# Four staging places in turn: where the block chunks of a down projection keep their output rows

## The chip, the cores and the metric

The kernel runs on one core of one Trainium2 chip. The metric is the time of one execution in microseconds (us) on the device. TensorE multiplies, VectorE (DVE in the profile) and ScalarE (ACT) do the work between the products, GpSimd (POOL) issues the transfers that accumulate, SyncE (SP) the plain ones.

## The reference, cut to what matters

One decoder layer runs on 576 tokens (512 of a prompt, 64 of a sample group): a combined Mamba2 and mLSTM mixer, a cross-attention over 256 memory rows, and a SwiGLU network. All is float32. The change touches only the last product of the last part:

```python
u = _rms(x) * g_pre_ffn
f = (jax.nn.silu(u @ w_gate) * (u @ w_up)) @ w_down      # 1024 -> 2816 -> 1024
x = x + _rms(f) * g_post_ffn
```

## The kernel before, in words

Activations lie with features on the 128 partitions and tokens along the free axis. Every float32 product is made of three: each operand is split into a high part, a cast to the fp32r type, and a low part, what the cast left over; a product is high times high, high times low and low times high (lines 1860 to 1862 for the down projection). So each weight tile and each operand needs a cast on ACT (line 192) and a difference on DVE (line 193).

The hidden width is 22 tiles of 128. The gated rows are made in pairs of tiles (`Pair`, called by the number of the pair's first tile: 4, 6, 8, ... 20). A pair multiplies 2x2 blocks with seven products instead of eight, the two 288-token halves `E[0]` and `E[1]` being one of the two block axes. The gate values of one pair are four blocks of 128x288 in the tile `gt`, which has room for two pairs: `gates(j)` returns half `j // 2 % 2` of it. When a pair is done, `place` forms differences of its four blocks (line 1611) and splits them into the operand tile `hop`.

The down projection runs in four pieces over the hidden axis. The middle two are the block chunks, `down_blocks(1)` behind pair 8 and `down_blocks(2)` behind pair 14. Each takes three operand tiles and gives all eight output rows of 128 features, as four blocks of two rows: `Down(c, n_)` for `n_` 0 to 3 is called block 0 to block 3 here. A block

- loads its weights into a `raw` and a `rawx` buffer (line 1821, on SP; two buffers of each, which `Pair` uses too, at lines 1651 and 1655),
- forms sums and differences of them (lines 1837 and 1611) and splits the results into `whi`/`wlo`, `wacc` and `u3h`/`u3l`,
- runs seven products of nine matmuls each, products 0 to 6, in up to three PSUM banks,
- moves intermediate banks out with `keep` (ACT, line 1865) into the small tiles `cc` and `ct`, and adds them to a later bank with `plus` (DVE, line 1868), whose result goes into the block's *staging rows* `s.st`: three of the four results of a block come by `plus`, the fourth is a copy on ACT (line 1907),
- adds the two staging rows to the sum in device memory, `f2_d`, with two accumulating transfers (`store`, line 1914, on POOL).

Block n's products 5 and 6 (`late`) come in the program after block n+1's products 0 and 1 (`early`). `Pair` objects are prepared in the same way around it, so the work of the first gated pair behind a chunk (pair 10 behind chunk 1, pair 16 behind chunk 2) is mixed into its last blocks.

Blocks 0 and 2 stage in two buffers of the tag "ssq" (tile `fst`), blocks 1 and 3 in one half of `gt`: that of the last pair ahead of the chunk, `gates(6 * c + 2)`, pair 8 for chunk 1 and pair 14 for chunk 2. A staging place that is used again waits until the transfers out of it have landed.

The order of the instructions in this part of the program is set by the tile scheduler from its own estimate of times, engine by engine; on the chip every engine then takes its instructions strictly in that order. Transfers issued from one engine start in that engine's order as well. One more user of the tag "ssq" follows: the tile `ssqf` for the last piece, whose padding POOL clears (line 1023) and which takes over the buffer of whichever block used the tag last.

The names in the profile: `ps_dn` is a PSUM bank of the down projection, `ps_g` and `ps_u` are those of a gated pair, `f_d` is `f2_d`.

Of the kernel before, what the change touches and what calls it, by code (L numbers as in the profile page):

```python
# [116 lines left out]
def build(nc, tc, ctx, I, O):  # L117
# [187 lines left out]
    for k in range(KT):  # L305
        if k % 2 == 0:
            c = slice(128 * k, 128 * k + 256)
# [1328 lines left out]
    def gates(j):  # L1636

        return [[gt[:, 4 * (j // 2 % 2) + 2 * a + i, :] for i in range(2)] for a in range(2)]
# [6 lines left out]
    class Pair:  # L1645

        def __init__(s, j, up, dst):
            s.j, s.up, s.dst, s.first = j, up, dst, not up and j in (10, 16)
            s.src = I["wup" if up else "wgate"]
            s.r1 = wp.tile([P, 1024], F32, name="raw", tag="raw", bufs=2)  # L1650
            S.dma_start(s.r1, s.src[j])
# [162 lines left out]
    class Down:  # L1814

        def __init__(s, c, n_):
            s.c, s.j = c, 2 * n_
            s.r1 = wp.tile([P, 1024], F32, name="raw", tag="raw", bufs=2)[:, :768]
            s.r2 = fp.tile([P, 1024], F32, name="rawx", tag="rawx", bufs=2)[:, :768]
            for a, r in enumerate((s.r1, s.r2)):  # L1820
                S.dma_start(r, I["wdown"][s.j + a, :, 768 * c - 256:768 * c + 512])
            if n_ % 2:
                g4 = gates(6 * c + 2)
                s.st = [[g4[a][i] for i in range(2)] for a in range(2)]
                s.rows = [gt[:, 4 * ((3 * c + 1) % 2) + 2 * a:4 * ((3 * c + 1) % 2) + 2 * a + 2, :].rearrange("p i t -> p (i t)") for a in range(2)]
            else:
                s.rows = [ph.tile([P, 640], F32, name="fst", tag="ssq", bufs=2)[:, :T] for _ in range(2)]
                s.st = [[r[:, c_] for c_ in E] for r in s.rows]
# [144 lines left out]
    with tc.manual_schedule(engines={TE.engine, A.engine, V.engine, G.engine, S.engine}):  # L1973
# [5 lines left out]
        gt = fp.tile([P, 8, 288], F32, name="gt")  # L1979
# [263 lines left out]
```

## Time and profile before

| | us |
|---|---|
| Median of 3 runs | 1169.33 (1166.7 to 1169.33) |
| The profiled execution | 1174.03 |
| its span, first to last instruction | 1172.2 |
| TensorE busy in the span | 1118.5 (95%), 8355 matmuls |
| DVE, ACT, POOL busy | 756.5 (65%), 619.8 (53%), 232.8 (20%) |
| Mean granted TensorE clock | 0.978 of full speed |

By stage, in us from the start of the span:

| stretch | what runs | TensorE busy | granted clock |
|---|---|---|---|
| 0 to 865 | everything up to pair 8 | 849.09 of 865 | 0.99 |
| 865 to 945 | chunk 1, start of pair 10 | 65.78 of 80 | 0.88 |
| 945 to 995 | pairs 10 to 14 | 50.00 of 50 | 0.99 |
| 995 to 1085 | chunk 2, pairs 16 and 18 | 72.69 of 90 | 0.89 |
| 1085 to 1172.2 | pair 20, last piece, output | 80.93 of 87.2 | 0.99 |

The busy time of TensorE is that of matmuls whose ends are modelled, so a full stretch is one without gaps, not one at peak. In the table the gaps stand in two places, the two block chunks. The third part of a timeline row in brackets is the idle time of the engine just before the instruction and what ended it.

### The profile page before, as it was taken

The numbers are of one execution on the slowest core, as the hardware profiler recorded it, in microseconds if no ns is written. First come the engines' busy times: TensorE is split into PE (matmuls) and PEld (weight loads), VectorE is DVE, ScalarE is ACT, GpSimd is POOL, SyncE is SP. The second block draws the span as 40 slices with busy tenths as digits, with TensorE's granted clock in tenths as the row PEclk, the third lists the DMA queues.
The fourth block names the chain that finished last, engine by engine and source line by source line (L and its number), as shares of the span: only waits on it lengthen the run. The fifth ranks groups of instructions, "written<-read, shape, count | busy, mean of one in ns | idle before, by whom it ended". The sixth has DMA issues, their size and how long they took to land.

```text
span 1172.2 us, 21300 instructions
## 1 busy us (share of the span) xinstructions
PE 1118.5 (95%) x8355; PEld 1062.3 (91%) x8355; DVE 756.5 (65%) x1503; ACT 619.8 (53%) x1148; POOL 232.8 (20%) x319
## 2 busy tenths in 40 slices
PE   9999999999999999999999999999998899778997
PEld 8999898898998999899888899999987899778997
DVE  6897773567766865677544556665583578554655
ACT  6877432445643656555444456346652475444654
POOL 1334534322121121100443011000101210021100
PEclk9999999999998999999999999999998989889999
DMA  6785565454544378834777556426724873278632
GB/s 210 167 156 123 146 172 162 123 139 126 173 122 136 90 251 279 290 96 152 230 264 254 206 160 230 159 81 182 180 76 98 190 152 96 66 164 223 151 135 81
DMA packets 61592, 190.21 MB, mean 162 GB/s; under 512 B 6796, under 2 KB 11020, under 8 KB 60852
## 3 DMA queue, kind: packets, MB, share of 16 engines
q1 hardware_dynamic: 43892, 142.19, 37.1%
q0 software_dynamic: 17312, 46.15, 19.3%
q8 instruction: 65, 1.06, 0.4%
q10 hardware_dynamic: 288, 0.52, 0.1%
q14 instruction: 35, 0.29, 0.1%
HBM read 159.52 MB, written 29.30 MB: 161 GB/s over the span
## 4 chain that ended last, share of the span: by engine, by line
PE 71%; DMA 12%; DVE 6%; issue 6%; ACT 5%; SPq 0%; POOL 0%; DVEq 0%; ACTq 0%; POOLq 0%
PE ps_in L201 5%; PE ps_in L203 5%; PE ps_in L202 5%; PE ps_o L201 2%; PE ps_o L203 2%; PE ps_o L202 2%; PE ps_g L1720 2%; PE ps_dn L201 2%; DMA rawx<-wgate 2%; PE ps_u L1720 2%; PE ps_u L1721 2%; PE ps_g L1721 2%; PE ps_g L1722 2%; PE ps_u L1722 2%; PE ps_dn L203 2%
## 5 line engine op out<-in xcount | busy, mean ns | idle before, releaser
L201 PE MATMUL ps_in<-uh,whi 128*128 128x320 f32 (+1 forms) x544 | 166.4, 306 | 0.0
L203 PE MATMUL ps_in<-uh,wlo 128*128 128x320 f32 (+1 forms) x544 | 163.7, 301 | 0.0
L202 PE MATMUL ps_in<-ul,whi 128*128 128x320 f32 (+1 forms) x544 | 163.2, 300 | 0.0
L181 ACT CAST whi<-raw 128x1024 fp32r<-128x1024 f32 (+1 forms) x102 | 102.8, 1011 | 78.6 <-PE ps_in L202 19.4
L188 DVE TENSOR_TENSOR wlo<-raw,whi 128x512 fp32r<-128x512 f32 (+1 forms) x94 | 88.0, 936 | 59.0 <-ACT whi L181 58.4
L201 PEld LDWEIGHTS ps_in<-uh,whi 128*128 128x128 f32 x544 | 104.1, 191 | 2.6 <-issue 1.2
L203 PEld LDWEIGHTS ps_in<-uh,wlo 128*128 128x128 f32 x544 | 103.9, 191 | 1.6 <-issue 1.3
L202 PEld LDWEIGHTS ps_in<-ul,whi 128*128 128x128 f32 x544 | 104.1, 191 | 0.7
L186 POOL DMA_DIRECT2D wlo<-win x32 | 28.4, 888 | 94.6 <-ACT wlo L185 84.2
L1720 PE MATMUL ps_u<-b,whi 128*128 128x288 f32 x144 | 42.8, 297 | 3.6 <-DVE gt L1868 3.0
L1720 PE MATMUL ps_g<-b,whi 128*128 128x288 f32 x144 | 43.1, 300 | 1.0 <-ACT cc L1778 0.8
L1721 PE MATMUL ps_g<-b,whi 128*128 128x288 f32 x144 | 42.8, 297 | 0.0
L1721 PE MATMUL ps_u<-b,whi 128*128 128x288 f32 x144 | 42.5, 295 | 0.0
L201 PE MATMUL ps_o<-mixm_h,whi 128*128 128x256 f32 (+1 forms) x128 | 38.8, 303 | 2.8 <-ACT whi L181 2.8
L201 PE MATMUL ps_xo<-qh,whi 128*128 128x288 f32 x128 | 37.9, 301 | 1.0 <-ACT f_xo L1407 1.0
L774 PE MATMUL ps_v<-wlo,uh 128*128 128x256 f32 x128 | 36.8, 291 | 1.9 <-DMA wlo<-wv 1.9
L202 PE MATMUL ps_o<-mixm_l,whi 128*128 128x256 f32 (+1 forms) x128 | 38.6, 302 | 0.0
L203 PE MATMUL ps_o<-mixm_h,wlo 128*128 128x256 f32 (+1 forms) x128 | 38.3, 303 | 0.0
L201 PE MATMUL ps_xq<-u2h,whi 128*128 128x320 f32 (+1 forms) x128 | 38.2, 303 | 0.0
L202 PE MATMUL ps_xq<-u2l,whi 128*128 128x320 f32 (+1 forms) x128 | 38.0, 298 | 0.0
L203 PE MATMUL ps_xq<-u2h,wlo 128*128 128x320 f32 (+1 forms) x128 | 37.9, 296 | 0.0
L203 PE MATMUL ps_xo<-qh,wlo 128*128 128x288 f32 x128 | 37.8, 296 | 0.0
(769 smaller groups left out, 3967.0 us busy)
## 6 DMA issues: line engine op xcount, KB each, us to landing
raw<-win SPq DMA_DIRECT2D x35, 512.0 KB, 3.8
raw<-wout SPq DMA_DIRECT2D x17, 512.0 KB, 4.4
kva<-kc SPq DMA_DIRECT2D x16, 512.0 KB, 7.0
kva<-vc SPq DMA_DIRECT2D x16, 512.0 KB, 6.3
raw<-wxq SPq DMA_DIRECT2D x13, 512.0 KB, 3.8
raw<-wgate SPq DMA_DIRECT2D x13, 512.0 KB, 6.8
raw<-wup SPq DMA_DIRECT2D x13, 512.0 KB, 4.2
wlo<-win POOLq DMA_DIRECT2D x24, 256.0 KB, 5.6
```

Of the source, the lines that this page charges most:

```text
L181: A.copy(hi[:, :n], raw[:, :n])
L186: G.dma_start(lo[:, a:b], src[:, a:b], accum_op=ALU.add)
L188: e.tensor_tensor(lo[:, a:b], raw[:, a:b], hi[:, a:b].bitcast(F32), op=ALU.subtract)
L201: mm(ps, wh, ah, start=i == 0, stop=False)
L202: mm(ps, wh, al, start=False, stop=False)
L203: m = mm(ps, wl, ah, start=False, stop=i == len(tiles) - 1)
L774: m = mm(o, ah, lo[:, j:j + 256], start=False, stop=k == KT - 1, skip_group_check=True)
L1720: mm(ps, wh, b[0][:, k, :], start=start and k == 0, stop=False, skip_group_check=True)
L1721: mm(ps, wh, b[1][:, k, :], start=False, stop=False, skip_group_check=True)
L1722: m = mm(ps, wl, b[0][:, k, :], start=False, stop=k == 3, skip_group_check=True)
```

## The change

The four blocks of a chunk stage their rows in another rotation. Blocks 0 and 3 use the two "ssq" buffers, block 1 one half of `gt`, block 2 the other: block 1 takes the half of the last pair but one ahead of the chunk (pair 6 for chunk 1, pair 12 for chunk 2), block 2 that of the last (pair 8, pair 14). The code gives this by `gates(6 * c + 4)` for block 1 and `gates(6 * c + 2)` for block 2. So within a chunk the "ssq" buffers serve twice still, but with two blocks between, and no half of `gt` serves twice. Shapes, numbers of instructions and transfers stay.

```diff
-            if n_ % 2:
-                g4 = gates(6 * c + 2)
+            if n_ in (1, 2):
+                g4, g0 = gates(6 * c + 6 - 2 * n_), 4 * ((3 * c + 3 - n_) % 2)
                 s.st = [[g4[a][i] for i in range(2)] for a in range(2)]
-                s.rows = [gt[:, 4 * ((3 * c + 1) % 2) + 2 * a:4 * ((3 * c + 1) % 2) + 2 * a + 2, :].rearrange("p i t -> p (i t)") for a in range(2)]
+                s.rows = [gt[:, g0 + 2 * a:g0 + 2 * a + 2, :].rearrange("p i t -> p (i t)") for a in range(2)]
             else:
                 s.rows = [ph.tile([P, 640], F32, name="fst", tag="ssq", bufs=2)[:, :T] for _ in range(2)]
                 s.st = [[r[:, c_] for c_ in E] for r in s.rows]
```

The built order of TensorE's and SP's instructions is the same before and after. On DVE one instruction moves in each chunk. Where chunk 1 begins, DVE forms pair 8's differences (`gt<-gt`) and the weight sums of the next blocks; the piece of the difference shows the first `plus` of block 1 come ahead of the weight sum of block 2:

```order
 L1611 TENSOR_TENSOR gt<-gt 128x288
 L193 TENSOR_TENSOR u3l<-raw,u3h 128x3x128
+L1868 TENSOR_TENSOR gt<-cc,ps_dn 128x288
 L1837 TENSOR_TENSOR sw<-rawx 128x384
 L1611 TENSOR_TENSOR gt<-gt 128x288
```

It stood behind the last of pair 8's differences, since it wrote into that pair's half; now it stands ahead of three of them. ACT's copy that depends on it (line 1865, block 2's product 0) moves up by two casts of `hop`.

The second place is DVE in the middle of chunk 1, from the split of block 2's weights to the first `plus` of block 3 (chunk 2 has the same rows). The numbers tell buffers apart; in brackets are the engines and DMA queues whose semaphores the instruction waits for. Before:

```order
L1868 TENSOR_TENSOR fst_10283<-cc_8891,ps_dn_10304 128x288 [waits DMASW4_49,DVE_49,PE_49]
L1837 TENSOR_TENSOR sw_8890<-rawx_10379 128x384 [waits DMAHW4_49]
L1868 TENSOR_TENSOR gt_8889<-cc_8891,ps_dn_10258 128x288 [waits Activation_49]
L1611 TENSOR_TENSOR sw_8890<-sw_8890,raw_10378 128x384 [waits DVE_49]
L1611 TENSOR_TENSOR rawx_10379<-raw_10378,rawx_10379 128x384
L1611 TENSOR_TENSOR raw_10378<-raw_10378,sw_8890 128x384 [waits DVE_49]
L193 TENSOR_TENSOR wlo_10389<-sw_8890,whi_10388 128x768 [waits Activation_49]
L1868 TENSOR_TENSOR gt_8889<-ct_7853,ps_dn_10258 128x288 [waits PE_49]
L1674 TENSOR_TENSOR wlo_10481<-raw_10475,whi_10479 128x1024 [waits DMAHW5_49,Activation_49]
L193 TENSOR_TENSOR wacc_10298<-rawx_10280,wacc_10297 128x768 [waits Activation_49]
L193 TENSOR_TENSOR u3l_7847<-raw_10378,u3h_7846 128x3x128 [waits Activation_49]
L1868 TENSOR_TENSOR gt_8889<-cc_8891,ps_dn_10401 128x288 [waits DMASW6_49,PE_49]
```

After:

```order
L1868 TENSOR_TENSOR gt_8889<-cc_8891,ps_dn_10302 128x288 [waits PE_49]
L1837 TENSOR_TENSOR sw_8890<-rawx_10377 128x384 [waits DMAHW4_49,DVE_49]
L1868 TENSOR_TENSOR gt_8889<-cc_8891,ps_dn_10258 128x288 [waits Activation_49]
L1611 TENSOR_TENSOR sw_8890<-sw_8890,raw_10376 128x384 [waits DVE_49]
L1611 TENSOR_TENSOR rawx_10377<-raw_10376,rawx_10377 128x384
L1611 TENSOR_TENSOR raw_10376<-raw_10376,sw_8890 128x384 [waits DVE_49]
L193 TENSOR_TENSOR wlo_10389<-sw_8890,whi_10388 128x768 [waits Activation_49]
L1868 TENSOR_TENSOR gt_8889<-ct_7853,ps_dn_10258 128x288 [waits PE_49]
L1674 TENSOR_TENSOR wlo_10481<-raw_10475,whi_10479 128x1024 [waits DMAHW5_49,Activation_49]
L193 TENSOR_TENSOR wacc_10296<-rawx_10280,wacc_10295 128x768 [waits Activation_49]
L193 TENSOR_TENSOR u3l_7847<-raw_10376,u3h_7846 128x3x128 [waits Activation_49]
L1868 TENSOR_TENSOR fst_10380<-cc_8891,ps_dn_10401 128x288 [waits DMASW4_49,PE_49]
```

No row moves here. Block 2's first `plus` (the first row) no longer names a DMA queue; block 3's (the last) names another one, that of block 0's transfer instead of block 1's.

The third place is POOL's queue at the end of chunk 2, from block 2's transfers on. Before:

```order
L1914 DMA f2_d_8133<-fst_11463 128x576 [waits DMASW4_49,DVE_49]
L1914 DMA f2_d_8133<-fst_11464 128x576 [waits DMASW5_49,Activation_49]
L1023 MEMSET ssqf_12408 128x64 [waits DMASW7_49,DMASW4_49]
L1667 DMA wlo_11781<-wup 128x512 [waits DMASW6_49,Activation_49]
L1667 DMA wacc_11777<-wup 128x1024 [waits DVE_49,Activation_49]
L1914 DMA f2_d_8133<-gt_8889 128x576 [waits DMASW0_49,DVE_49,Activation_49]
L1667 DMA wacc_11903<-wgate 128x1024 [waits DMASW1_49,PE_49,Activation_49]
L1914 DMA f2_d_8133<-gt_8889 128x576 [waits DMASW2_49,DVE_49]
L1667 DMA wacc_12029<-wup 128x1024 [waits DMASW7_49,DMASW3_49,Activation_49]
```

After:

```order
L1914 DMA f2_d_8133<-gt_8889 128x576 [waits DMASW4_49,DVE_49]
L1914 DMA f2_d_8133<-gt_8889 128x576 [waits DMASW5_49,Activation_49]
L1667 DMA wlo_11781<-wup 128x512 [waits DMASW6_49,Activation_49]
L1667 DMA wacc_11777<-wup 128x1024 [waits DMASW7_49,DVE_49,Activation_49]
L1914 DMA f2_d_8133<-fst_11561 128x576 [waits DMASW0_49,DVE_49,Activation_49]
L1667 DMA wacc_11903<-wgate 128x1024 [waits DMASW1_49,PE_49,Activation_49]
L1914 DMA f2_d_8133<-fst_11560 128x576 [waits DMASW2_49,DVE_49]
L1023 MEMSET ssqf_12408 128x64 [waits DMASW0_49]
L1667 DMA wacc_12029<-wup 128x1024 [waits DMASW7_49,DMASW3_49,Activation_49]
```

The clearing of `ssqf` goes from behind block 2's transfers to behind block 3's, since block 3 is now the last to use its buffer.

## The prediction

> **What bounds the kernel now.** I read the stages first (the table above): TensorE has gaps only in the two block chunks, 865 to 945 and 995 to 1085 us. Then, of the waits there, what TensorE stood for longest: four stalls on ACT's copy at line 1865, two in each chunk. Its timeline has them, with the idle time in brackets:
>
> ```profile
> 895.36 0.61 PE L1860 MATMUL ps_dn<-hop,wacc 128*128 128x288 f32 x1 [3.35 <-ACT cc L1865]
> 910.49 0.40 PE L1860 MATMUL ps_dn<-hop,wacc 128*128 128x288 f32 x1 [3.41 <-ACT cc L1865]
> ...
> 1021.40 0.61 PE L1860 MATMUL ps_dn<-hop,wacc 128*128 128x288 f32 x1 [3.32 <-ACT cc L1865]
> 1036.30 0.61 PE L1860 MATMUL ps_dn<-hop,wacc 128*128 128x288 f32 x1 [4.58 <-ACT cc L1865]
> ```
>
> Each is at product 5 of a block, which may not add to its bank until ACT has kept the bank's value. The cause of the first stall, and the way on to the second, stand in the chain of waits:
>
> ```profile
> 888.40 5.60 DMA f_d<-fst
> ...
> 894.90 0.41 ACT cc L1865
> ...
> 900.46 1.22 DVE wlo L1674
> 901.68 0.88 DVE wacc L193
> 902.57 6.84 DMA rawx<-wgate
> ```
>
> Block 0's rows leave its two buffers from 888.40. Block 2's first sum goes into the same buffers, so DVE stands until the transfer has landed; ACT's copies stand behind DVE, and TensorE behind ACT. Then the chain runs through DVE's split of pair 10's first weights and the split into `wacc`, which frees a `rawx` buffer, to the load that takes it, and through this load to the second stall. DVE's timeline, and ACT's cast of those weights:
>
> ```profile
> 894.12 0.45 DVE L1868 TENSOR_TENSOR fst<-cc,ps_dn 128x288 f32<-128x288 f32 x1 [4.49 <-DMA f_d<-fst]
> 894.49 0.55 DVE L1837 TENSOR_TENSOR sw<-rawx 128x384 f32<-128x384 f32 x1
> ...
> 905.31 0.46 DVE L1868 TENSOR_TENSOR gt<-cc,ps_dn 128x288 f32<-128x288 f32 x1 [2.29 <-DMA f_d<-gt]
> 909.51 0.69 DVE L1677 TENSOR_TENSOR sw<-rawx 128x512 f32<-128x512 f32 x1 [3.75 <-DMA rawx<-wgate]
> ...
> 897.03 1.04 ACT L1671 CAST whi<-raw 128x1024 fp32r<-128x1024 f32 x1
> ```
>
> DVE was free from 894.12 - 4.49 = 889.63. Chunk 2 repeats it all about 126 us later.
>
> **The change, part by part.**
>
> *Block 2's first sum* goes into the half of `gt` that pair 8 has left, and names no transfer any more, so DVE's 4.49 us of waiting go. What is late next? The instruction behind it, `sw<-rawx`, needs block 3's weights. SP issued that load, and after it pair 10's first weights:
>
> ```profile
> 888.83 0.33 SPq L1821 DMA_DIRECT2D rawx<-wdown  x1
> 889.66 0.33 SPq L1651 DMA_DIRECT2D raw<-wgate  x1
> ...
> raw<-wgate SPq DMA_DIRECT2D x1, 512.0 KB, 6.5
> rawx<-wdown SPq DMA_DIRECT2D x1, 384.0 KB, 3.7
> ...
> q1 hardware_dynamic: 144, 0.39, 49.3%
> ...
> q1 hardware_dynamic: 144, 0.52, 33.9%
> ```
>
> The two rows with KB are the same loads in chunk 2, where the profile gives the time to landing (3.7 and 6.5 us; issued at 1014.90 and 1015.73). The last two are the MB of the plain queue in 889 to 893 and in 893 to 897 of chunk 1. They agree: 888.83 + 3.7 = 892.5, with 0.39 MB (the 384 KB) moved by 893, and 889.66 + 6.5 = 896.2, with the 512 KB moved after it. So `sw` starts at 892.6 instead of 894.49: 1.9 us of the 4.49. When TensorE had the bank of block 2's product ready no row here tells; had it come only at 892.01, where TensorE's work ended (895.36 - 3.35), DVE would still be at `sw` by 892.5.
>
> *TensorE.* ACT's copy stands only behind product 4 now, which ended at 892.01. From ACT's start to the matmul it took 895.36 - 894.90 = 0.46, so TensorE goes on at 892.5: 2.9 us of the stall go. The 18 matmuls of products 5 and 6 ran at half clock: 0.25 us each by the row at 894.70 below (6.14 us for 25), against 0.13 at full clock (the row at 945.90, 49.10 for 373), so 4.4 us become 2.4. TensorE is through with block 1 at 894.9 instead of 899.8, 4.9 us earlier.
>
> *What sets the next stall.* This gain ends at the load of 902.57, which waits for DVE's two splits. The first needs ACT's cast of `raw`, and `raw` lands at 896.2. ACT casts from 896.25 to 897.3 (1.04), only 0.8 us earlier than before; DVE splits until 898.55 (1.22) and 899.45 (0.88), and the load leaves there instead of at 902.57. **Chunk 1: 3.1 us.** TensorE meets the same cast (pair 10's first product is mixed in behind product 6): a new gap from 894.9 to 897.35, covered by the second stall, which only begins earlier.
>
> *Chunk 2.* `raw<-wgate` lands at 1015.73 + 6.5 = 1022.2; plus 1.04, 1.20 and 0.88, with the small steps between them, makes 1025.4, against
>
> ```profile
> 1025.79 1.20 DVE wlo L1674
> 1026.99 0.88 DVE wacc L193
> 1027.89 7.34 DMA rawx<-wgate
> ```
>
> **Chunk 2: 2.4 us** (1027.89 - 1025.45). Behind these loads every load hangs on the one before (a split frees the buffer), up to the gapless stretches, so both shifts should last: 5.5 together.
>
> *Block 3's first sum* loses its wait of 2.29 us at 905.31, in both chunks. I cost this at nothing: DVE's next instruction stands until 909.51 for the load. Without that cover it would be 2.3 each. Its new place, block 0's buffers, was free at 894.12 (the first) and, with the second transfer about as long, by 896; the sum comes at 899.9.
>
> *Block 1's first sum*, moved to the chunk's head, takes 0.45 us of DVE (as in the row at 894.12) ahead of splits that TensorE waits for there. Bounds per chunk 0 and 0.45; I take 0.15, nearer to nothing, since DVE saves the same 0.45 a few instructions later: 0.3 in all.
>
> *POOL's clearing* stands behind block 3's transfers now and waits for the first of them; behind it is a `wacc` transfer:
>
> ```profile
> 1064.98 0.86 POOL L1667 DMA_DIRECT2D wacc<-wup  x1 [8.62 <-ACT wacc L1666]
> ```
>
> That row waited 8.62 us for ACT's cast, so POOL stood free from 1056.4. The clearing costs only what the landing is later than the cast; I take nothing, and as the other bound 0.5.
>
> *The sum:* 3.1 + 2.4 - 0.3 = 5.2 us off. The profiled execution (1174.03, span 1172.2) would come to 1168.8. It lies 4.7 above the median of the runs, which these stalls do not explain, so I take the same 5.2 off the median: **1164.1**.
>
> *The clock* is left at zero in the sum and goes into the range. Stretches, with TensorE's busy time and matmuls first, and last the granted clock, the share of the DMA engines in use and GB/s:
>
> ```profile
> 881.00:884.40 3.40, 3.40 (x16) 3.40 (x16) 1.82 (x3) 0.84 (x2) 0.00 (x0) 0.50 0.00 0
> 894.70:901.50 6.80, 6.14 (x25) 6.14 (x26) 4.53 (x8) 4.33 (x8) 0.67 (x2) 0.50 0.22 46
> 915.00:930.00 15.00, 13.45 (x93) 12.33 (x93) 9.63 (x16) 7.27 (x12) 6.18 (x7) 1.00 0.93 212
> 939.00:945.90 6.90, 6.11 (x25) 6.11 (x26) 3.96 (x6) 4.18 (x9) 1.50 (x2) 0.51 0.81 161
> 945.90:995.00 49.10, 49.10 (x373) 49.10 (x372) 39.30 (x78) 32.41 (x60) 4.33 (x5) 1.00 0.53 123
> ```
>
> A stretch at half clock behind a stall lasts 3.4 or 6.8 us. The one from 939.00 opens the gapless stretch, where it costs time: 25 matmuls at 0.25 instead of 0.13, 3.0 us. Starting elsewhere it may be the shorter kind, 1.4 us less; at chunk 2's end it may turn longer, 1.7 more. Both ends go into the range. The Trainium skill, "TensorE: Matmul & The Clock Gate", section "Part 1: The HAM clock gate", says the gate decides by windows of 3413 ns that run free of the program, full clock coming back after a busy one. The two lengths in the trace agree with one and two such windows; by that rule the cost of 3.0 would become anything from 1.7 to 3.4 with the new start, and chunk 1 would give 2.7 to 4.4, as an estimate, instead of 3.1.
>
> **Rivals.**
>
> *The loads give it back* (no change): behind the second stall the transfers fill the engines, so loads that leave earlier only meet more of the accumulating transfers, which come forward too. For it: the share of 0.93 from 915. Against: from 894.7 to 901.5 it is 0.22, idle time that the earlier load uses. If all of chunk 2's 2.4 and a fifth of chunk 1's go, 5.2 - 2.4 - 0.6 = 2.2 stay: 1167.1.
>
> *TensorE's own gain lasts* (faster still): if `raw<-wgate` lands two us earlier than it did, the full 4.9 of chunk 1 counts, and in chunk 2 the stall's 3.32 less 0.5 and the same 2.0 of clock, 4.8: 9.7 less 0.3, so 1159.9. For it: the chain goes from the stall to DVE's splits through TensorE and names this load nowhere. Against: its bytes moved until 893 to 897, and nothing in the change sends it earlier.
>
> *A slow transfer holds what was free of it* (slower). Pair 10's first gate value (DVE, line 1730) goes into the half of `gt` that block 1 now stages in, and waits for block 1's transfers; on DVE behind it are the next weight sums, and the loads hang on those. The same holds for pair 16.
>
> ```profile
> 918.04 0.46 DVE L1730 TENSOR_TENSOR gt<-ps_g,cc 128x288 f32<-128x288 f32 x1 [1.00 <-PE ps_g L1722]
> ...
> DMA to landing us min/median/max: 4.4/8.2/10.5
> ```
>
> The sums end by 896 and ACT's copy by 898.5, so the transfers leave by 899; the gate comes at 918.04 - 3.1 = 914.9. It begins to cost at 16 us from issue to landing, eats the gain of both chunks at 18.6 and makes the kernel slower by 0.3% at some 20.4 in each: 1173. Against: the longest landing of transfers out of `gt` was 10.5 (second row).
>
> *The change keeps the wait*, since blocks 0 and 3 still share buffers: block 3's sum would then wait for block 0's second transfer. There are some 3 us between them, and behind the sum a load is waited for anyway; it would end as the forecast.
>
> **How the numbers follow.** The forecast has 0.62 (its own range, with the clock and a load's landing off by a us or two, 1161 to 1167.5), the loads that give it back 0.20, TensorE's own gain 0.11, slower 0.07. For the range, 1159 takes in the second rival, and 1168.5 most of the first; about 0.15 is left out. Within 0.3%, 3.5 us, is about what a measurement of this kernel tells from no change. Faster by more are nine tenths of the forecast, the second rival and a little of the first, 0.68; the same 0.25; slower 0.07.
>
> **What would show it.** Right: block 2's first sum without a wait for `f_d<-fst`, and then about 2.5 us of DVE's waiting at `sw` for `rawx<-wdown`; the first stall of each chunk near 0.5 us, and a new one of some 2 us on ACT's cast at line 1671; from SP's `rawx<-wdown` to its `rawx<-wgate` 10.6 us instead of 13.7 (902.57 - 888.83) in chunk 1, and 10.5 instead of 13.0 in chunk 2; the second stall as long as before or longer; everything behind it as far from that load as it was. Wrong: block 2's sum still waits, or the first stall stays above 2 us; the way from that load to the gapless stretch grows by what the load gained (first rival); `raw<-wgate` lands well under 6.5 us (second); a wait for `f_d<-gt` at line 1730 (third).

## The result and the profile after

The changed kernel takes 1157.5 us (median of 14 runs, 1152.7 to 1169.0) beside 1169.33 of the kernel before (14 runs): a ratio of 0.9905, with a 95% interval of 0.9879 to 0.9931. So it is 11.1 us faster (0.0095 x 1169.33), where the prediction had 5.2, and it lies 1.5 us below the lower end of the range. A second set of 6 runs, with no edit, gave 0.9897 (0.985 to 0.9943). The profiled execution of the first set took 1158.21 us:

```profile
core 0: 1156.4 us, clock 0.989
```

This lies 0.7 above its median, while the one before (1174.03) lay 4.7 above its own. So 4 of the 15.8 us between the two profiles are not the change's; each term is taken below from as many profiles as there are.

The steps of the change show as they were worked out. DVE's timeline of the changed kernel in chunk 1, with the idle time in brackets:

```profile
888.40 0.45 DVE L1868 TENSOR_TENSOR gt<-cc,ps_dn 128x288 f32<-128x288 f32 x1
891.31 0.56 DVE L1837 TENSOR_TENSOR sw<-rawx 128x384 f32<-128x384 f32 x1 [2.46 <-DMA rawx<-wdown]
...
895.97 1.23 DVE L1674 TENSOR_TENSOR wlo<-raw,whi 128x1024 fp32r<-128x1024 f32 x1 [1.03 <-ACT whi L1671]
...
898.68 0.45 DVE L1868 TENSOR_TENSOR fst<-cc,ps_dn 128x288 f32<-128x288 f32 x1 [0.15 <-PE ps_dn L1862]
904.27 0.69 DVE L1677 TENSOR_TENSOR sw<-rawx 128x512 f32<-128x512 f32 x1 [5.13 <-DMA rawx<-wgate]
```

At 888.40 stands the first sum of block 2, with no wait; 2.46 us of waiting follow at `sw` for block 3's weights; block 3's first sum (898.68) waits 0.15 instead of 2.29, and all of that is spent at 904.27, for the load. TensorE, both chunks:

```profile
891.29 0.40 PE L1860 MATMUL ps_dn<-hop,wacc 128*128 128x288 f32 x1 [0.54 <-ACT cc L1865]
895.99 0.40 PE L1720 MATMUL ps_g<-u3h,whi 128*128 128x288 f32 x1 [1.77 <-ACT whi L1671]
905.25 0.40 PE L1860 MATMUL ps_dn<-hop,wacc 128*128 128x288 f32 x1 [2.90 <-ACT cc L1865]
...
1009.77 0.40 PE L1860 MATMUL ps_dn<-hop,wacc 128*128 128x288 f32 x1 [0.54 <-ACT cc L1865]
1014.54 0.40 PE L1720 MATMUL ps_g<-u3h,whi 128*128 128x288 f32 x1 [1.79 <-ACT whi L1671]
1023.54 0.40 PE L1860 MATMUL ps_dn<-hop,wacc 128*128 128x288 f32 x1 [1.12 <-ACT cc L1865]
```

The first stall is 0.54 us, the new gap on ACT's cast 1.8. The second stall, though, is shorter than before: 2.90 and 1.12 instead of 3.41 and 4.58. SP's loads, first of the kernel before and then of the changed one:

```profile
902.57 0.33 SPq L1655 DMA_DIRECT2D rawx<-wgate  x1
915.60 0.33 SPq L1655 DMA_DIRECT2D rawx<-wup  x1
```

```profile
887.57 0.33 SPq L1821 DMA_DIRECT2D rawx<-wdown  x1
898.09 0.33 SPq L1655 DMA_DIRECT2D rawx<-wgate  x1
910.36 0.33 SPq L1655 DMA_DIRECT2D rawx<-wup  x1
```

From `rawx<-wdown` to `rawx<-wgate` it takes 898.09 - 887.57 = 10.52 us, where the prediction had 10.6. But from there to the next `rawx<-wup` it takes 12.27 instead of 13.03; in chunk 2 it is 11.04 (1016.64 to 1027.68) instead of 14.22 (1027.89 to 1042.11). The prediction took this stretch as unchanged. One reason stands in POOL's timeline, where block 1's two accumulating transfers leave; before, and then after:

```profile
900.83 1.76 POOL L1914 DMA_DIRECT2D f_d<-gt  x2 [10.51 <-DVE gt L1868]
```

```profile
895.23 0.86 POOL L1914 DMA_DIRECT2D f_d<-gt  x1 [6.15 <-DVE gt L1868]
897.26 0.86 POOL L1914 DMA_DIRECT2D f_d<-gt  x1 [1.17 <-ACT gt L1907]
```

Before, both leave as a pair 1.74 and 1.20 us ahead of the load (902.57); now 2.86 and 0.83 ahead of it (898.09). The chain of waits gives the load 6.08 us instead of 6.84:

```profile
888.41 6.46 DMA raw<-wgate
894.89 1.05 ACT whi L1671
895.97 1.23 DVE wlo L1674
897.19 0.88 DVE wacc L193
898.09 6.08 DMA rawx<-wgate
```

The granted clock is the other candidate: the profile of before has nine stretches at half clock in the two chunks, 41 us in all, this one three, 13.6 us. A second profile of each kernel has five, 27.3 us before and 17.1 after, so the first pair overstates the difference. Columns as in the prediction:

```profile
906.20:909.60 3.40, 3.40 (x16) 3.37 (x16) 2.51 (x5) 3.11 (x5) 0.00 (x0) 0.50 0.44 77
...
1015.40:1018.80 3.40, 3.40 (x16) 3.40 (x15) 1.92 (x4) 0.83 (x3) 0.86 (x1) 0.50 0.92 107
1063.20:1070.00 6.80, 5.31 (x22) 5.31 (x23) 6.47 (x13) 5.57 (x10) 1.73 (x2) 0.50 0.41 60
```

### The profile page after: what moved, and what is told of

Read it like the earlier page. It is cut to its first block, busy times and chain, and to the rows that moved or that the text cites. A ratio compares the mean times of both kernels' runs of the same rounds, so it can differ in the third digit from the quotient of the medians.

```text
span 1156.4 us, 21306 instructions
## 1 busy us (share of the span) xinstructions
PE 1109.2 (96%) x8355; PEld 1051.9 (91%) x8355; DVE 756.5 (65%) x1503; ACT 619.3 (54%) x1148; POOL 231.9 (20%) x319
## 4 chain that ended last, share of the span: by engine, by line
PE 69%; DMA 14%; DVE 8%; ACT 5%; issue 3%; POOL 1%; SPq 0%; DVEq 0%; ACTq 0%; POOLq 0%
PE ps_in L201 5%; PE ps_in L203 5%; PE ps_in L202 5%; PE ps_o L201 2%; PE ps_o L203 2%; PE ps_u L1720 2%; PE ps_o L202 2%; PE ps_u L1721 2%; PE ps_u L1722 2%; DMA raw<-wgate 2%; PE ps_dn L201 2%; PE ps_dn L203 2%; DMA rawx<-wgate 2%; PE ps_dn L202 2%; PE ps_g L1720 2%
```

## The experiments

Ratios are to the kernel before, run on the same chip, with 95% intervals. The edits shown are shortened, and their comments are the document's. "The load" is `rawx<-wgate` of pairs 10 and 16, "the sum" DVE's line 1677 that waits for it (a line or two lower in kernels with added lines).

**The kernel before, once more (again).**

> The kernel before once more, with no edit: it gives the granted clock of every one of its runs, beside those of the changed kernel (0.984 to 0.993, 1152.7 to 1169.0 us). Clock theory (the part of the gain that the forecast missed, 11.8 - 5.2 = 6.6 us, is TensorE running less of its time at half clock): the clock here is lower by about 0.005 on the mean of the runs (6.6 of 1160 us), in each kernel the time goes with the clock at about 1.2 us per 0.001, and at the same clock the two kernels differ by about 5. Load theory (the loads of chunk 2 come forward further than forecast, and the clock is worth nothing): clocks alike within 0.002, and at the same clock the kernels differ by 10 to 12.

0.9994 (0.9973 to 1.0016). The mean granted clock is 0.9839 over 35 runs of the kernel before and 0.9846 over these 12, against 0.9890 over the 14 of the changed one. Within each kernel a line through its runs gives 1.1 to 1.2 us per 0.001, and at the same clock before and after differ by 4.1 us, with a standard error of 0.8. All of this is what the clock theory expected. They are a correlation, though: a run that stands longer shows a lower clock as well as the other way round. The fills below were meant to tell the two apart; what does is the comparison of chunks further down. The second profile of before is also the measure of what varies:

```profile
901.06 0.33 SPq L1655 DMA_DIRECT2D rawx<-wgate  x1
...
899.33 1.75 POOL L1914 DMA_DIRECT2D f_d<-gt  x2 [9.75 <-DVE gt L1868]
...
908.16 0.69 DVE L1677 TENSOR_TENSOR sw<-rawx 128x512 f32<-128x512 f32 x1 [3.11 <-DMA rawx<-wgate]
```

Block 1's transfers are again 1.73 us ahead, and from the load to the sum it takes 7.10.

**One chunk at a time (c1_only, c2_only).**

```diff
-            if n_ % 2:
+            if n_ in ((1, 2) if c == 1 else (1, 3)):   # c2_only: c == 2; block 1 of the other chunk stays with block 3
```

> The change in chunk 1 alone; chunk 2 stages as before. As forecast: 3.1 - 0.15, so 3.0 us faster than before. Clock theory: 5 to 6 faster, with the granted clock up by about 0.002 to 0.003. Load theory (what was missed lies in chunk 2's loads): 3.0 faster.

> The change in chunk 2 alone. As forecast: 2.4 - 0.15, so 2.3 us faster. Clock theory: about 5 to 6 faster, clock up by 0.002 to 0.003. Load theory: 8 to 9 faster (all that was missed lies here), whatever the clock.

0.9957 (0.9931 to 0.9982), 5.0 us, and 0.9965 (0.9941 to 0.9988), 4.1 us. Each chunk has about half of the gain. Both lie above what the forecast gave them (3.0 and 2.3), but either interval reaches down to it (2.1 and 1.4 us). The theory that all that was missed lies in chunk 2, which asked for 8 to 9 us there, falls.

**Block 3's place alone (b3_only), block 2's alone (b2_only).**

```diff
-            if n_ % 2:                    # b3_only                 b2_only: if n_ > 0:
+                q = 6 * c + 5 - n_        # pair whose half is used           q = 6 * c + 4 - 2 * (n_ % 2)
```

> In both chunks blocks 1 and 3 are staged in places of their own in the gates' halves, and blocks 0 and 2 share the staging rows as before: block 3's first sum loses its wait of 2.29 us, block 2's keeps its wait of 4.49. As forecast: nothing, or 0.3 slower (block 1's sum moves to the head here too). Theory that block 3's wait was not covered: 2.3 faster in each chunk, 4.6 in all.

> Block 2 alone gets a place of its own (in the other half of the gates' tile); blocks 1 and 3 share a half and blocks 0 and 1 are as before, so block 3's wait for block 1 stays. The first gate value of pairs 10 and 16 now waits for block 2's transfers, and moves behind the next weight sums on DVE. If block 2's sum carries the whole gain: 0.990 to 0.993 of before (less block 1's 0.3), with the clock up by 0.004 to 0.005. If block 3's place matters beside it: a third to a half of the gain. If the gate value's wait for block 2's transfers costs: 0.995 to 1.000.

0.9995 (0.9971 to 1.0019) without block 3's wait, and 0.9903 (0.9867 to 0.9939) without block 2's. Block 2's sum carries all of it; block 3's wait, and block 1's sum at the head of the chunk, are worth nothing that can be measured.

**Matmuls of zeros, to keep the clock up (bfill, afill9, afill_all, afillb).**

```diff
+        zf = fp.tile([P, 288], BF16, name="zf"); V.memset(zf, 0.0)
+        fill = lambda ps, n, first=False: [mm(ps[:, 0:288], zf[:, 0:128], zf, start=first, stop=first, skip_group_check=True) for _ in range(n)]
...
         def early(s):                                 # of Pair: afill9, afill_all
             s.x, y = s.bank(), s.bank()
+            fill(s.x, {(10, 0): 9, (16, 0): 9}.get((s.j, s.up), 0), True)      # afill_all: and (12, 0): 8, (18, 1): 24
...
         def end(s):                                   # of Down
+            fill(s.z, {(1, 1): 20, (2, 1): 20}.get((s.c, s.j // 2), 0))        # bfill
-            s.mul(s.x, 4, 5, start=False)
+            m = s.mul(s.x, 4, 5, start=False)
+            with tc.issue_after(m.ins): fill(s.z, {(1, 2): 8, (2, 2): 6}.get((s.c, s.j // 2), 0))   # afillb
```

> The kernel before, staging as before, with 20 extra matmuls of zeros (128x288, bf16, added to the bank of product 3) ahead of product 5 of block 1 in each chunk, so that TensorE works for 20 x 0.13 = 2.6 us of the first stall instead of standing. Block 2's first sum still waits 4.5 us. Clock theory: no half-clock stretch behind the first stall (two windows in chunk 1, one in chunk 2, by the profile), so the mean clock is up by 0.003 to 0.0045 and the time down by 3.5 to 5 us at 1.17 us per 0.001. Staging theory (the waits alone make the gain, the half clock only shows where TensorE stood): no change in the time, whatever the clock.

> The changed kernel with 9 such matmuls of zeros ahead of the first product of pairs 10 and 16 (gate), where TensorE stands 1.77 and 1.79 us now. Clock theory: that gap turns the clock down in about half of the cases (in the profile in chunk 2, not in chunk 1), so the mean clock is up by 0.001 to 0.0015 and the time down by 1 to 2 us against the changed kernel, 0.990 of before or a little less. Staging theory: as the changed kernel, 0.9905 of before.

> As the one before, and 8 more ahead of the first product of pair 12's gate (a wait of 2.22 us in the changed kernel) and 24 ahead of that of pair 18's up (4.61 us, a stretch of 6.8 us at half clock behind it, and TensorE without a gap from there to the end). The matmuls in the plan move some of ACT's, DVE's and POOL's steps of pair 18 by a place or two. Clock theory: a further 2 to 3.5 us less, some 1153 to 1155, with the clock at 0.992 or above. Staging theory: 1157, or more where the 24 outlast the wait.

The first two miss their place. The matmuls were ready early and were issued early, some 14 us ahead of the first stall in the one and 4 us ahead of the gap in the other (first and last start, by the tile of zeros; bfill, then afill9):

```profile
L1982 PE MATMUL ps_dn<-zf x40: 286/286/297, 875.3 to 1000.2; 128*128 128x288 bf16 x40
```

```profile
L1982 PE MATMUL ps_g<-zf x18: 286/286/297, 888.5 to 1007.7; 128*128 128x288 bf16 x18
```

They gave 0.9985 (0.9959 to 1.0012) and 0.9919 (0.9891 to 0.9947) and do not test the clock. The first shows that 2.6 us more of TensorE's work at the head of each chunk has no cost that can be measured, with the first stall still 3.35 us. The third reached a mean clock of 0.9910, the highest seen, and was not faster than the changed kernel for it: 0.9917 (0.9886 to 0.9948). But some of its steps of pair 18 had changed places, and 14 of the 24 matmuls meant for the wait of pair 18 ran behind that wait, where TensorE has no gap from there to 1151 us:

```profile
1068.46 2.17 PE L1982 MATMUL ps_u<-zf 128*128 128x288 bf16 x14
```

They added 2.17 us of work there. By the slope of 1.17 us per 0.001 its clock (0.9910 against 0.9887 over the changed kernel's 20 runs) would be worth 2.7 us, as an estimate, so the two about cancel, and the run does not speak against the clock. The fourth was queued behind product 4 and did stand in the second stall:

> The changed kernel with 8 (chunk 1) and 6 (chunk 2) matmuls of zeros behind product 4 of block 2, so in the second stall, which is 2.90 and 1.12 us long there. From the landing of rawx<-wgate to the next rawx<-wup it takes 5.12 us in some profiles and 6.1 to 6.8 in others, where TensorE's products 5 and 6 run at half clock. Clock theory: 5.12 more often, 1 us less in a chunk where the fill keeps the clock up, so 0.5 to 1.5 us faster than the changed kernel, with the mean clock up by 0.001. Rival (the clock there costs nothing): as the changed kernel, or slower by what the matmuls outlast the stall in chunk 2 (under 0.5 us).

```profile
904.85 0.40 PE L1860 MATMUL ps_dn<-hop,wacc 128*128 128x288 f32 x1 [1.62 <-ACT cc L1866]
...
932.80:939.60 6.80, 6.08 (x25) 6.08 (x26) 3.89 (x6) 4.08 (x9) 1.43 (x2) 0.50 0.83 164
```

What is left of the stall is 1.62 us (first row), no half clock follows right behind it, and from the sum to the next `rawx<-wup` it takes 5.11 us in both chunks. The time is 0.9925 (0.9897 to 0.9953), no less than the changed kernel's. But the mean clock did not rise: it is 0.9879 over its 12 runs, and in this profile the half clock came later, for 6.8 us from 932.80 (second row). So none of the four fills is a clean test of the clock.

**Block 1's transfers held back (hold1, b3_hold).** POOL copies one column of the landed load, and the two transfers are queued behind the copy; no other engine's order changes.

```diff
             S.dma_start(s.r2, s.src[s.j + 1])
+            g = G.tensor_copy(tiny, s.r2[:, 0:1])      # pairs 10 and 16
+            with tc.issue_after(g.ins): block1.store(1); block1.store(0)
```

> The changed kernel with block 1's two transfers held on POOL until the load rawx<-wgate of pair 10 (16) has landed. Theory of the transfers in the way: the load takes 5 to 5.6 us instead of 6.1, so 1 to 2 us faster than the changed kernel in all (0.989 of before), unless pair 10's first gate value, which goes into block 1's place, now waits for them: issued at 904.3 and landing some 6 us later, at 910.5, against 912.7. Rival: as the changed kernel.

> Blocks 1 and 3 in places of their own, blocks 0 and 2 sharing the staging rows as before (which alone gave 0.9995 of before: block 2's sum still waits 4.5 us), and block 1's two transfers held until the load rawx<-wgate has landed. Theory of the transfers in the way: this load takes 5 to 6 us instead of 7.5, with the first stall kept whole, so 2.5 to 4.5 us faster than before, 0.996 to 0.998. Rival: 0.9995, no change.

The load's time is theirs. In hold1:

```profile
899.13 0.33 SPq L1655 DMA_DIRECT2D rawx<-wgate  x1
909.14 0.33 SPq L1655 DMA_DIRECT2D rawx<-wup  x1
...
903.59 1.76 POOL L1926 DMA_DIRECT2D f_d<-gt  x2 [0.31 <-issue]
...
903.13 0.69 DVE L1679 TENSOR_TENSOR sw<-rawx 128x512 f32<-128x512 f32 x1 [1.42 <-DMA rawx<-wgate]
915.32 0.69 DVE L1679 TENSOR_TENSOR sw<-rawx 128x512 f32<-128x512 f32 x1 [3.67 <-DMA rawx<-wup]
```

From the load to the sum 903.13 - 899.13 = 4.0 us, against 6.18 in the changed kernel (904.27 - 898.09); in b3_hold 4.36, against 7.47 in the kernel with block 3's place alone. But held back, the transfers meet the next load: `rawx<-wup` takes 915.32 - 909.14 = 6.2 us, where the changed kernel has 4.4 (910.36 to DVE's next `sw` at 914.72). In chunk 2 the same load takes 7.05, and pair 16's first gate value waits 1.08 us for the held transfers. hold1 comes to 0.9925 (0.9899 to 0.995), no gain; b3_hold to 0.9972 (0.9946 to 0.9998), 3.3 us, with block 2's wait kept whole.

**Block 1's transfers right at the load (late2, late_h1).** The same with the copy of a column of pair 10's first low parts (DVE's split at line 1674), or of its high parts (ACT's cast at line 1671).

> The changed kernel, but block 1's two accumulating transfers (line 1914) are held on POOL until DVE's split of pair 10's (16's) first weights has ended, some 0.8 us ahead of the load rawx<-wgate, about where they stand in the kernel before (1.74 and 1.19 us ahead of it there; 2.9 and 0.8 ahead in the changed kernel). A copy of one column on POOL does the holding; no other engine's order changes. Theory of the transfers in the way (in the profiles so far this load takes 6.9 to 8.0 us from issue to DVE's start where the staging is as before, 5.9 to 6.2 where it is changed, because block 1's rows leave earlier against it): the load takes 7 us or more again, and the kernel is 2 to 3 us slower than the changed one, 0.9925 to 0.993 of before. Rival (the load's time has another cause, and what the forecast missed is the clock alone): as the changed kernel, 0.990.

> The changed kernel with block 1's two transfers held on POOL until ACT's cast of pair 10's (16's) first weights (line 1671) has ended: by the profile of the kernel held until the split, POOL's copy then ends 0.85 us later, so they are issued 1.3 and 0.7 us ahead of the load rawx<-wgate, nearly as in the kernel before (1.74 and 1.19). If they are what made the load slow before, and its time counts: the load 7 us or more, the kernel 2 to 3 us slower than the changed one. If the load is slow but the time does not count (what is lost there is taken back behind it): the load 7 us, the time as the changed kernel's. If something else made the load slow: 6 us and no change.

> Once more the changed kernel with block 1's transfers held until DVE's split of pair 10's first weights, so that they are issued with the load and not ahead of it (load 5.3 and 4.0 us in its profile, no second stall). If the load's time counts: 2 to 3 us faster than the changed kernel on the same chip. If not: the same within 1 us.

> The changed kernel once more with no edit, as the measure for the two beside it and for a second profile: some 0.990 of before, the load at 5.7 to 6.2 us, from its landing to the next rawx<-wup 5.12 us or 6.1.

Neither undid the change, since POOL's copy ended later than I had reckoned; late2, then late_h1:

```profile
900.22 0.33 SPq L1655 DMA_DIRECT2D rawx<-wgate  x1
...
900.18 1.75 POOL L1926 DMA_DIRECT2D f_d<-gt  x2
...
905.53 0.69 DVE L1679 TENSOR_TENSOR sw<-rawx 128x512 f32<-128x512 f32 x1 [2.75 <-DMA rawx<-wgate]
```

```profile
901.13 0.33 SPq L1655 DMA_DIRECT2D rawx<-wgate  x1
...
900.23 1.75 POOL L1926 DMA_DIRECT2D f_d<-gt  x2
...
906.50 0.69 DVE L1679 TENSOR_TENSOR sw<-rawx 128x512 f32<-128x512 f32 x1 [2.87 <-DMA rawx<-wgate]
```

In chunk 1 the load takes 5.3 and 5.4 us, less than in the changed kernel. Over the profiles, each chunk read as in these rows (afill_all, with steps in other places, is left out; its two chunks have 5.71 and 5.76):

| kernels (chunks) | block 1's two transfers, from the load | load to sum, us |
|---|---|---|
| block 2 staged as before (10) | 1.74 and 1.13 to 1.20 ahead | 6.94 to 8.04, mean 7.33 |
| block 2 in a place of its own (12) | 2.74 to 3.04 and 0.82 to 0.83 ahead | 5.63 to 6.52, mean 5.97 |
| late_h1 (2) | 0.9 and 0.36 ahead | 5.37, 5.08 |
| late2, twice (4) | 0.04 ahead, 0.5 behind | 5.31, 3.99, 5.28, 3.91 |
| hold1, b3_hold (4) | 4.5 to 6.6 behind | 4.00, 3.77, 4.36, 5.36 |

And here the load's time seems to count: late2 gave 0.9884 (0.9847 to 0.9921) and 0.9871 (0.9824 to 0.9919), late_h1 0.9869 (0.9818 to 0.992), after_again 0.9897 (0.985 to 0.9943). The mean of the 12 runs of late2 is 1155.3, that of the changed kernel's 20 is 1158.5: 3.3 us, with a standard error of 1.3. The load is shorter by 5.97 - 4.62 = 1.35 in each of two chunks, 2.7. So late2 is faster than the kernel before and probably faster than the changed one, though its interval overlaps the changed kernel's; on the one chip where both ran beside each other (6 runs each) the means differ by 3.0 us, with a standard error of 2.2.

## Why the prediction was right, and where it failed

*The way from DVE's wait to the load* was right for the profiled execution. From `rawx<-wdown` to `rawx<-wgate`, 13.74 and 12.99 us became 10.52 and 10.58, 5.6 in all, where the terms 3.1 and 2.4 made 5.5. `sw` waited 2.46 (about 2.5 was said), the first stall is 0.54 (0.5), the new gap 1.8 (2).

The prediction counted the half clock behind the first stall for TensorE alone; it did not see how much of this way is half clock too. Twelve chunks on record keep block 2's wait of 4.4 to 4.5 us and a first stall of 3.25 to 3.39 (those of the kernel before, again, b3_only, bfill and b3_hold, and the unchanged one of c1_only and of c2_only). The way takes 13.6 to 13.8 us in six of them, with 6.8 us at half clock behind the stall; 13.0 in four, with 3.4 us; and 11.69 in two, with none. Two of them in full, chunk 2 of the kernel before and then of b3_only (the stretches with TensorE's busy time and matmuls, the granted clock, the DMA engines' share and GB/s):

```profile
1014.90:1027.89 12.99, 9.67 (x63) 0.87 0.54 119
...
1020.16 0.45 DVE L1868 TENSOR_TENSOR fst<-cc,ps_dn 128x288 f32<-128x288 f32 x1 [4.45 <-DMA f_d<-fst]
...
1025.40 0.46 DVE L1868 TENSOR_TENSOR gt<-ct,ps_dn 128x288 f32<-128x288 f32 x1 [1.25 <-PE ps_dn L1862]
```

```profile
1010.09:1021.78 11.69, 8.35 (x62) 1.00 0.59 132
...
1015.37 0.45 DVE L1869 TENSOR_TENSOR fst<-cc,ps_dn 128x288 f32<-128x288 f32 x1 [4.47 <-DMA f_d<-fst]
...
1019.30 0.45 DVE L1869 TENSOR_TENSOR gt<-ct,ps_dn 128x288 f32<-128x288 f32 x1
```

The wait for the transfer is the same. The sum ahead of DVE's split needs product 6 of block 1: with products 5 and 6 partly at half clock DVE waits 1.25 us for it, at full clock not at all. In the ten such chunks of the table the way takes 13.1 us on the mean, in the twelve with a place of its own for block 2 10.6, wherever the half clock falls. So the change gains 2.5 us a chunk here, 5.0 in all. By the chunks at full clock 1.1 of it (11.69 - 10.6) is the wait alone, and 1.4 is half clock taken off the path.

*Block 3's wait at nothing* was right (0.9995 without it), and *block 1's sum* of 0.3 is too small to be seen in that run. *POOL's clearing* cost nothing: it stands at 1044.28, and the `wacc` transfer behind it still waits for ACT's cast.

```profile
1044.28 0.15 POOL L1023 MEMSET ssqf<- 128x64 f32 x1 [2.52 <-DMA f_d<-fst]
1046.55 0.86 POOL L1667 DMA_DIRECT2D wacc<-wup  x1 [2.12 <-ACT wacc L1666]
```

*What failed is the step "Behind these loads every load hangs on the one before ..., so both shifts should last: 5.5 together".* The shifts lasted, but the load itself was carried over at its old 6.84 and 7.34 us. It became 1.36 us shorter in each chunk (7.33 to 5.97), 2.7 in all. Block 1's two transfers come out of products 5 and 6, which the first stall had held back. Before, DVE's last sum of block 1 (900.09) is ready after ACT's copy (898.72), and both transfers leave together behind it. After, that sum comes at 894.49 and releases the first, while the copy for the second stands in ACT's order behind the cast that waits for `raw<-wgate` (894.89 in the chain above):

```profile
896.58 0.39 ACT L1907 COPY gt<-ps_dn 128x288 f32<-128x288 f32 x1
```

So they leave spread out, and one of them is well under way when the load is issued. The runs with held transfers show that they set the load's time, with the rest of the traffic as it is; b3_hold (3.3 us) and late2 (3.3, standard error 1.3) point to this time reaching the end of the program. The prediction had seen that the accumulating transfers "come forward too", and counted it against the gain only, as its first rival. One of the two came forward further than the load (2.86 us ahead of it instead of 1.74), the other less (0.83 instead of 1.20), and together this helped it.

The two engines' queues share the transfer engines meanwhile: while the load is in flight, they are in use for 0.97 and 1.00 of the time, before and after.

```profile
902.57:909.42 6.85, 4.51 (x35) 4.28 (x33) 0.90 (x2) 0.00 (x0) 0.02 (x1) 1.00 0.97 230
```

```profile
898.09:904.17 6.08, 4.26 (x33) 4.03 (x31) 0.89 (x2) 0.00 (x0) 0.03 (x1) 1.00 1.00 243
```

The Trainium skill, "DMA: Bandwidth & Descriptors", section "Queues, rings and completion order", says that each DMA engine takes turns, packet by packet, between the queue rows that have work for it. The table is in line with that, though it doesn't show the turns themselves: the load pays for what POOL's queue has in flight beside it, 7.33 us with the pair just ahead of it and 4.0 and 3.77 in hold1 with none.

*The clock, left at zero in the sum, is the second step that failed.* The range had it at the start of the gapless stretches; it acts inside the chunks as well. Besides the 1.4 us a chunk above, there is the way from the sum to the next `rawx<-wup`: 6.48 us on the mean of the ten chunks staged as before, and 5.48 in ten with a place of its own for block 2 (the fills afill_all and afillb left out). The values come in steps (5.12; 5.95 to 6.29; 6.79), by how many of TensorE's matmuls run at half clock there: in the changed kernel's profile 6.09 in chunk 1, with the stretch at 906.20 in it, and 5.12 in chunk 2 without one. That is 1.0 a chunk, 2.0 in all.

Together 5.0 + 2.7 + 2.0 = 9.7 us are found on the path, of the 11.1 measured; the interval of the measurement is 8.1 to 14.1. Some 4.8 of the 9.7 are half clock (1.4 and 1.0 in each chunk), and the other 4.9 stand beside the 4.1 by which the two kernels differ at the same clock (standard error 0.8). That these chunks differ with the stall the same says that here the clock makes the time and is not only a sign of standing. No run changed the clock alone, though, so its share of the end time is worked out, not measured.

*The rivals.* The loads did not give the gain back: from `rawx<-wup` of chunk 1 to `rawx<-wdown` of chunk 2 it takes 96.0 to 96.3 us with block 2 staged as before and 95.0 to 95.9 with its own place, in the profiles where no half clock falls there; from `rawx<-wup` of chunk 2 to the end it takes 128.1 to 130.2 and, in the changed kernel's two profiles, 128.7 and 129.6. hold1 shows that they can, once the transfers stand in the way of the next one. TensorE's own gain did not last: `raw<-wgate` landed 6.46 us after its issue, as forecast, and the new gap followed. The gate value of pair 10 did not wait for a transfer:

```profile
912.67 0.46 DVE L1730 TENSOR_TENSOR gt<-ps_g,cc 128x288 f32<-128x288 f32 x1 [0.87 <-PE ps_g L1722]
```

And the change did take the wait away. The range left out a transfer that gets shorter, and half clock inside the chunks: neither was bounded from the side of the gain.

## What to carry to other kernels

When a stall is removed, list the transfers that it held back as well as the instructions, and put each against the load that sets the next stall: the load's old duration includes what was in flight beside it, and is not a constant that can be moved along. In this kernel the load on the path was cheapest when bulky transfers that nobody waits for soon left with it or behind it, as long as they didn't reach the next load on the path. A stall can also cost more than its length: ask which work runs at half clock behind it, and who waits for that work; several profiles of the same kernel show it. And before a matmul is added to keep the clock up, look in the trace where it was issued: an instruction that is ready early runs early.

## What had not been expected of the hardware

The same 512 KB load takes from 3.8 to 8.0 us here, by when two transfers of 288 KB were issued on another engine's queue: the worst is a pair 1.2 to 1.7 us ahead of it, and a pair issued with it (0.04 ahead) leaves it at 3.9 and 4.0 in chunk 2, as in hold1 with none (3.77), but at 5.3 in chunk 1. What else has a part in it was not tried: b3_hold has 5.36 in chunk 2 with neither transfer ahead.

The same stall of TensorE, 3.25 to 3.39 us long, was followed by 6.8 us at half clock in six chunks, by 3.4 in four and by none in two, and the way from `rawx<-wdown` to `rawx<-wgate` went with it: 13.7, 13.0 and 11.69 us. A gap of 1.77 us (895.99) was followed by no stretch at half clock, one of 1.79 (1014.54) by 3.4 us of it, in the same profile. So the length of the gap alone does not decide it.
